# A plain column order in the first matmul behind the scan, and two scaled blocks moved behind the last sums

## The chip, the cores and the metric

The kernel runs on one core of one Trainium2 chip. The metric is the device time of one execution in microseconds. The kernel before takes 1699.45 us, the median of three runs (1698.41 to 1699.90).

## What is computed

The trunk has one layer here (`DEPTH = 1`), so the reference comes down to an attention branch between two norms:

```python
x1   = rms_norm(x, norm_attn)                      # 256 rows, 4096 columns, float32
proj = x1 @ w_in                                   # 4096 x 16384 -> q | k | v | gate
o    = stick_breaking_attention(q, k, v)           # 32 heads of 128, strictly causal
h    = x + (o * silu(gate)) @ w_out                # 4096 x 4096
out  = rms_norm(h, final_norm)
```

In a head, `z = q k' / sqrt(128)`, the weight of position s for row t is `sigmoid(z[t,s])` times the product of `1 - sigmoid(z[t,j])` over s < j < t, and the kernel forms that product as a sum of logarithms: the "scan" over positions, which TensorE does with a triangle of ones as one operand.

## The kernel before

**Tiling.** The rows are two blocks, t = 0 (rows 0-127) and t = 1 (rows 128-255). The columns of `w_in` are worked in 16 units of two heads (q, k, gate and v columns of both), those of `w_out` in 4 units. A unit runs over 16 steps of 256 of the 4096 summed elements. In a step the 2 x 2 x 2 block products are done as eight plain products or, in most steps, as seven by sums and differences of blocks. Each product adds a 128x512 result into one PSUM bank (`acc`).

**One product is three matmuls.** Every float32 operand is split into a rounded high part and the rest (`wh`, `wl` for the weights; `sh`, `sl` or `oh`, `ol` for the rows). `mm3` (line 813) issues high x high, high x low, low x high, each 128x512. The profile writes them `acc<-wh,sh`, `acc<-wl,sh`, `acc<-wh,sl`.

**The order of columns.** A matmul may take its 512 columns in any order, if it reads and writes them in the same one. A word of three letters gives the order of a product's three matmuls. "e" takes groups of eight neighbouring columns: the first group of each 32 columns, then the second of each 32, in four rounds. "c" does the same with groups of four and of each 16 columns. Which word a product gets is set in `product` (line 1234): it counts the products since other matmuls ran (`since_others`). The first seven behind such matmuls get the words of `BEHIND_OTHERS` (line 37). Later the first product of a step gets "cce" or "ecc", and all others "eee".

**The other matmuls.** `ten` (line 345) issues the groups of the attention between products and sets the count to zero. A head has four groups: `turn` (transposes of q and k), `scores` (z), `scan` (line 879: four matmuls with the triangle and a transpose of the gate), and `out_of_head` (line 909: the sum over v, and a transpose). There are 32 heads, so 32 scans, all while `w_in`'s products and the first of `w_out`'s run.

**Order of the work.** A planner written in the kernel (`Plan`) simulates the engines with its own costs when the program is built, and emits each engine's instructions in the order in which they would start. Each piece of work has a due time as its key; a piece that is not ready is passed over, and on the chip each engine then runs its own queue strictly in that order.

**The end.** The last five parts are finished bank by bank (`LAST_ORDER`), so that rows 128-255 are complete first: their sums, squares, mean, root (`part_done`, `finish`) and scaling (`rows_out`, line 1201) run while TensorE still works on rows 0-127. The last bank (3, rows 0-127) is added in two halves of 256 columns. `joined` (line 1173) then makes the mean but for the last 256 columns and tells `("most", t)`; `finish` waits for that, takes the root on ScalarE, one Newton step on VectorE, and starts `rows_out` for the eight blocks of 512 columns of that t. Blocks 6 and 7 still lack the gain and are scaled by one VectorE instruction with two factors; the others by VectorE or ScalarE. Each block then goes out by a DMA that SyncE issues.

Of the kernel before, what the change touches and what calls it, by code (L numbers as in the profile page):

```python
# [19 lines left out]
P = 128  # L20
# [13 lines left out]

ROUNDS = 4
RUNS = {"e": 8, "c": 4}
BEHIND_OTHERS = ("ccc", "ecc", "eee", "eee", "eee", "eee", "cce")
IN_STEP = ("cce", "ecc")
WARM, IDLE = 10, 640
# [69 lines left out]
def tensor_ns(n):  # L109
    return 0.4167 * n + 8.5 if n > 128 else 109.0  # L110
# [138 lines left out]
def kernel(  # L249
# [10 lines left out]
    nc = Plan(tc)  # L260
# [50 lines left out]
    for g, (n, k) in enumerate(order):  # L311
        p = parts[n]
# [17 lines left out]
    def dve(emit, n, key=None, more=0, **kw):  # L330
        n = n if isinstance(n, tuple) else (n,)
        cost = sum(vector_ns(m) for m in n) + 122 * (len(n) - 1) + more
        return nc.work("vector", cost, emit, soon() if key is None else key, **kw)

    def act(emit, n, key=None, **kw):
        n = n if isinstance(n, tuple) else (n,)
        cost = sum(scalar_ns(m) for m in n) + 100 * (len(n) - 1)
        return nc.work("scalar", cost, emit, soon() if key is None else key, **kw)
# [1 line left out]

    FULL_P, FULL_S = (P,) * 2, (W,) * 2

    since_others = 0

    def ten(emit, *n):
        def others():
            nonlocal since_others
            since_others = 0
            emit()

        return nc.work("tensor", 40 + sum(tensor_ns(m) for m in n), others, nc.here - 1e4, wait=400)

    def moved(engine, emit, sizes, key, after=None, hold=False, adds=False, wait=0):
        issue = 550 if engine == "gpsimd" else 330
        return nc.work(
            engine, issue * len(sizes), emit, key, after=after, hold=hold, moves=[(4 * P * n, adds) for n in sizes],
            wait=wait,
        )
# [454 lines left out]
    def mm3(out_, a, b, start, stop, orders):  # L813

        (ah, al), (bh, bl) = a, b
        for k, (x, y) in enumerate(((ah, bh), (ah, bl), (al, bh))):
            to, y = (t.rearrange("p (h q e) -> p q h e", q=ROUNDS, e=RUNS[orders[k]]) for t in (out_, y))
            nc.tensor.matmul(to, x, y, start=start and k == 0, stop=stop and k == 2, skip_group_check=True)


    BW = 3 * P
    not_before = off.broadcast_to([P, 2, P])

    def head(u, i):
# [3 lines left out]
        def turn():  # L828
            for k in range(2):
                for t in range(NT):  # L830
                    c = k * CW + i * P
                    nc.tensor.transpose(tr[:, k, t * P : (t + 1) * P], st["qk", u][:, t, c : c + P], ident)

        yield ten(turn, P, P, P, P)
        if i == HG - 1:
            nc.give("one")
# [10 lines left out]
        def scores():  # L847
# [4 lines left out]
            nc.tensor.matmul(diagonal, ident_b, not_before, start=False, **kw)  # L852

        yield ten(scores, *FULL_P, *FULL_S, 2 * P)
        nc.give("gh")
        yield nc.take("gh", sooner=True)
# [22 lines left out]
        def scan():  # L879
# [4 lines left out]
            nc.tensor.matmul(z[:, 2 * P : BW], neg_one, fl[:, 0:P], stop=True, **kw)  # L884
            turned(gT, 0)

        yield ten(scan, BW, BW, P, P, P)
        nc.give("gh", "gh")
        if i == 0:
            yield nc.take("gh", sooner=True)  # L890
# [34 lines left out]
    def heads(u):  # L925
        nc.start(gate(u))
        yield nc.until(("qk", u))
        for i in range(HG):
            yield from head(u, i)

        nc.tell(("heads", u))
        if u < NS - 1:
            spill[u] = dp.tile([P, 4, P], F32, name=f"spill{u}")
            yield moved(
                "gpsimd", lambda: nc.gpsimd.dma_start(spill[u], st["o", u]), [4 * P], soon(),
                after=lambda: (nc.give("gh"), nc.tell(("spilled", u))),
            )
# [46 lines left out]
    hs, xres, grow = {}, {}, {}  # L984
# [186 lines left out]
    most = {}  # L1171
# [8 lines left out]
    def finish(last, t, late):  # L1180
        v, r, f = (scalar_of_rows() for _ in range(3))
        second = ssq_h[:, t, NJ : NJ + 1]

        def root():
            nc.scalar.activation(r, second, AF.Ln, scale=1.0 / D, bias=most[t])
            nc.scalar.activation(r, r, AF.Exp, scale=-0.5)

        yield act(root, (1, 1), late - 2)

        def factor():  # L1190
            nc.vector.scalar_tensor_tensor(
                out=v, in0=second, scalar=1.0 / D, in1=most[t], op0=ALU.mult, op1=ALU.add
            )
            e = newton(r, v, f"rout{t}")
            nc.vector.tensor_tensor(out=f, in0=r, in1=e, op=ALU.mult)

        yield dve(factor, (1, 1, 1, 1), late - 2)
        for k, c in enumerate(range(NJ)):
            nc.start(rows_out(c, t, f, late + 100 * (NT - t) + k))

    def rows_out(c, t, f, key):
        h = hs[c, t]
        if c >= NJ - 2:
            yield nc.until(("grow", c))
            yield dve(
                lambda: nc.vector.scalar_tensor_tensor(
                    out=h, in0=h, scalar=f, in1=grow[c], op0=ALU.mult, op1=ALU.mult
                ),
                W, key,
            )  # L1210
        elif c in ON_SCALAR[t]:
            yield act(lambda: nc.scalar.activation(h, h, AF.Copy, scale=f), W, key)
        else:
            yield dve(
                lambda: nc.vector.tensor_scalar(out=h, in0=h, scalar1=f, scalar2=None, op0=ALU.mult), W // 2, key
            )
        yield moved("sync", lambda: nc.sync.dma_start(out[t * P : (t + 1) * P, c * W : (c + 1) * W], h), [W], key)
# [16 lines left out]
    def product(n, k):  # L1234
        nonlocal since_others
        p = parts[n]
        b, f, c = p["prods"][k]
        h, l = forms[p["s"]]
        orders = "eee"
        if since_others < len(BEHIND_OTHERS):  # L1240
            orders = BEHIND_OTHERS[since_others]
        elif p["i"] == 0 and k == 0:
            orders = IN_STEP[p["s"] % len(IN_STEP)]
        since_others += 1
        mm3(
            ev[p["u"]][b],
            (h[:, PLACES[f], :], l[:, PLACES[f], :]),
            tuple(t[:, c].rearrange("p i n -> p (i n)") for t in (wh[n], wl[n])),
            starts[p["u"], b] == (n, k),
            ends[p["u"], b] == (n, k),  # L1250
            orders,
        )

    def products():
        for g, (n, k) in enumerate(order):
            p = parts[n]
            u, s = p["u"], p["s"]
            b, f, c = p["prods"][k]
            if u < 1:
                what = "s"  # L1260
            elif u < OUT0:
                what = "n"
            elif u == OUT0:
                what = "o"
            else:
                what = "r" if u == LAST and s in EIGHT_LAST else "p"
            if starts[u, b] == (n, k):
                yield nc.take(f"b{b}")
                ev.setdefault(u, {})[b] = acc.tile([P, W], F32, tag=f"b{b}", name=f"acc{u}_{b}")
            yield nc.until(("low", n, c), ("form", what, s), lead=nc.LEAD)  # L1270
            yield nc.work(
                "tensor", PRODUCT, lambda: product(n, k), g * PRODUCT, after=lambda n=n, k=k: done(n, k), hold=False
            )
            nc.here = g * PRODUCT
# [59 lines left out]
```

## Time and profile before

| | |
|---|---|
| runs, median (lowest to highest) | 1699.45 us (1698.41 to 1699.90) |
| the profiled execution | 1698.9 us |
| its span, first to last instruction | 1697.1 us |
| TensorE busy | 1680.2 us, 99%, 7776 matmuls |
| VectorE busy | 1602.0 us, 94% |
| ScalarE busy | 1206.7 us, 71% |
| granted TensorE clock, mean | 0.997 |
| DMA | 412.77 MB, 243 GB/s |

PE is TensorE's matmuls, PEld its weight loads, DVE VectorE, ACT ScalarE, POOL GpSimd, SP SyncE. The timeline gives for each instruction its start and its time in microseconds from the start of the span. A matmul's end is modelled and runs into the next one, so the rate of TensorE is read from the distance between two starts, not from the busy share. The profile shows shapes, not the order of columns: that is read from the kernel's code, by counting products behind a group of other matmuls. The kernel issues nearly everything through one helper, so all rows name line 132 and are told apart by their tiles: `z` is the bank of scores and scan, `o` the bank of a head's result, `acc` the products, `h` the rows of the result, `sq` the squares, `scalars` the means, roots and factors.

### The profile page before, as it was taken

To read this page: it belongs to the slowest core of one execution; us is meant where nothing else is said; L and a number is where in the kernel's file an instruction comes from. 1 tells how busy PE (TensorE), PEld (TensorE's weight loads), DVE (VectorE), ACT (ScalarE), POOL (GpSimd) and SP (SyncE) were. 2 spreads that over 40 slices of the span, in tenths; PEclk is the share of its full clock that TensorE was granted. 3 is DMA by queue.
4 is the path that set the end of the run, shared out by engine and by line. 5 is a ranking of instruction groups with operands and counts; after the bars stand their busy time and mean duration, and the time that the engine had idled before them with its cause. 6 is when DMAs were issued, how large, how long until landed. Compare 5 with 4: busy or idle time off the path is not lost.

```text
span 1697.1 us, 25128 instructions
## 1 busy us (share of the span) xinstructions
PE 1680.2 (99%) x7776; PEld 1417.4 (84%) x7776; DVE 1602.0 (94%) x2025; ACT 1206.7 (71%) x1665; POOL 324.9 (19%) x400
## 2 busy tenths in 40 slices
PE   9999999999999999999999999999999999999997
PEld 7888888888888888888888888888888888888885
DVE  8899999999999999999999999999999978999997
ACT  8986767676767676767676767676868775656654
POOL 0012222121222222222212121212122111212110
PEclk9999999999999999999999999999999999999998
DMA  9978888878787878797978797979797978888895
GB/s 343 332 197 247 232 247 222 252 217 253 215 256 212 256 212 266 199 272 196 276 201 269 198 268 196 272 198 269 204 264 210 300 230 266 245 245 256 246 304 185
DMA packets 248438, 412.77 MB, mean 243 GB/s; under 512 B 28016, under 2 KB 72560, under 8 KB 248304
## 3 DMA queue, kind: packets, MB, share of 16 engines
q1 hardware_dynamic: 194544, 354.24, 62.7%
q0 software_dynamic: 53472, 56.65, 20.0%
q8 instruction: 61, 1.00, 0.2%
q14 instruction: 73, 0.60, 0.1%
q10 hardware_dynamic: 288, 0.28, 0.1%
HBM read 402.93 MB, written 8.13 MB: 242 GB/s over the span
## 4 chain that ended last, share of the span: by engine, by line
PE 94%; DVE 3%; DMA 1%; issue 1%; ACT 1%; SPq 0%; DVEq 0%; ACTq 0%
PE acc L132 89%; PE z L132 3%; PE o L132 1%; DVE wl L132 1%; PE tr L132 1%; DVE h L132 1%; DVE raw L132 0%; ACT wh L132 0%; DMA raw<-in_w_out_dram 0%; DMA raw<-in_w_in_dram 0%; DMA xres<-in_x_dram 0%; SPq L132 0%; ACT sq L132 0%; DVE scalars L132 0%; DVE qk_sb L132 0%
## 5 line engine op out<-in xcount | busy, mean ns | idle before, releaser
L132 ACT CAST wh<-raw 128x1024 fp32r<-128x1024 f32 (+1 forms) x989 | 919.3, 970 | 385.5 <-DVE raw L132 160.9
L132 DVE TENSOR_TENSOR wl<-raw,wh 128x1024 fp32r<-128x1024 f32 (+1 forms) x815 | 975.7, 1220 | 49.3 <-ACT wh L132 23.9
L132 PE MATMUL acc<-wh,sh 128*128 128x512 f32 x2048 | 771.9, 389 | 0.1
L132 PE MATMUL acc<-wh,sl 128*128 128x512 f32 x1898 | 727.1, 383 | 1.8 <-DVE sl L132 1.8
L132 PE MATMUL acc<-wl,sh 128*128 128x512 f32 x1748 | 668.9, 383 | 0.1
L132 PEld LDWEIGHTS acc<-wh,sh 128*128 128x128 f32 x2048 | 384.0, 188 | 77.9 <-DVE qk_sb L132 4.9
L132 POOL DMA_DIRECT2D raw<-in_w_in_dram x300 | 258.3, 947 | 972.2 <-DMA raw<-in_w_in_dram 375.1
L132 PEld LDWEIGHTS acc<-wh,sl 128*128 128x128 f32 x1898 | 356.0, 188 | 66.3 <-DVE sl L132 2.4
L132 PEld LDWEIGHTS acc<-wl,sh 128*128 128x128 f32 x1748 | 328.4, 188 | 55.6 <-DVE wl L132 0.4
L132 DVE TENSOR_TENSOR raw<-raw,raw 128x512 f32<-128x512 f32 x348 | 238.3, 688 | 15.3 <-DMA raw<-in_w_in_dram 11.7
L132 PE MATMUL acc<-wh,oh 128*128 128x512 f32 x512 | 192.4, 383 | 0.0
L132 PE MATMUL acc<-wh,ol 128*128 128x512 f32 x488 | 186.7, 383 | 0.0
L132 PE MATMUL acc<-wl,oh 128*128 128x512 f32 x464 | 177.6, 383 | 1.4 <-DVE wl L132 1.4
L132 DVE TENSOR_TENSOR wh<-raw,wh 128x512 fp32r<-128x512 f32 x174 | 119.7, 688 | 3.3 <-ACT wh L132 2.7
L132 DVE TENSOR_TENSOR raw<-raw 128x512 f32<-128x512 f32 x174 | 119.4, 686 | 0.0
L132 PEld LDWEIGHTS acc<-wh,oh 128*128 128x128 f32 x512 | 96.1, 188 | 17.3
L132 PEld LDWEIGHTS acc<-wh,ol 128*128 128x128 f32 x488 | 91.5, 188 | 16.1
L132 PEld LDWEIGHTS acc<-wl,oh 128*128 128x128 f32 x464 | 87.1, 188 | 17.6 <-DVE wl L132 2.2
L132 POOL DMA_DIRECT2D raw<-in_w_out_dram x48 | 41.5, 984 | 173.8 <-DMA raw<-in_w_out_dram 85.2
L132 ACT ACTIVATE f<-f 128x384 f32<-128x384 f32 x96 | 50.5, 526 | 3.0
L132 POOL DMA_DIRECT2D p<-spill x27 | 17.0, 676 | 89.9 <-DVE ol L132 32.0
L132 DVE SCALAR_TENSOR_TENSOR gv_sb<-acc,scalars,gv_sb 128x512 f32<-128x512 f32 x45 | 33.5, 745 | 0.0
(86 smaller groups left out, 765.7 us busy)
## 6 DMA issues: line engine op xcount, KB each, us to landing
raw<-in_w_in_dram SPq DMA_DIRECT2D x1024, 256.0 KB, 4.5
raw<-in_w_out_dram SPq DMA_DIRECT2D x256, 256.0 KB, 4.5
raw<-in_w_in_dram POOLq DMA_DIRECT2D x300, 128.0 KB, 5.2
p<-spill POOLq DMA_DIRECT2D x27, 256.0 KB, 4.6
raw<-in_w_out_dram POOLq DMA_DIRECT2D x48, 128.0 KB, 5.4
xr<-in_x_dram SPq DMA_DIRECT2D x16, 256.0 KB, 5.3
xres<-in_x_dram SPq DMA_DIRECT2D x16, 256.0 KB, 5.5
out_dram<-h SPq DMA_DIRECT2D x16, 256.0 KB, 2.8
```

What stands on the lines that cost most here:

```text
L132: return self.tc.keep_in_program_order(getattr(self.engine, name)(*args, **kw))
```

## The change

Behind a scan, and only there, the words of the first two products change from "ccc", "ecc" to "rcc", "eee". The letter "r" is not in `RUNS`: `mm3` then leaves the 512 columns in their plain order. The words from the third product on stay as they were. In `rows_out`, blocks 6 and 7 wait for `("most", 0)` beside their gain. For rows 0-127 that has been told by then; for rows 128-255 it places the two instructions behind rows 0-127's last sums and `joined` on VectorE.

```diff
+BEHIND_SCAN = ("rcc", "eee")
 BEHIND_OTHERS = ("ccc", "ecc", "eee", "eee", "eee", "eee", "cce")
...
-    since_others = 0
-
-    def ten(emit, *n):
+    since_others, words = 0, BEHIND_OTHERS
+
+    def ten(emit, *n, behind=BEHIND_OTHERS):
         def others():
-            nonlocal since_others
-            since_others = 0
+            nonlocal since_others, words
+            since_others, words = 0, behind + BEHIND_OTHERS[len(behind) :]
             emit()
...
         for k, (x, y) in enumerate(((ah, bh), (ah, bl), (al, bh))):
-            to, y = (t.rearrange("p (h q e) -> p q h e", q=ROUNDS, e=RUNS[orders[k]]) for t in (out_, y))
+            if orders[k] in RUNS:
+                to, y = (t.rearrange("p (h q e) -> p q h e", q=ROUNDS, e=RUNS[orders[k]]) for t in (out_, y))
+            else:
+                to = out_
...
-        yield ten(scan, BW, BW, P, P, P)
+        yield ten(scan, BW, BW, P, P, P, behind=BEHIND_SCAN)
...
         if c >= NJ - 2:
-            yield nc.until(("grow", c))
+            yield nc.until(("grow", c), ("most", 0))
...
-        if since_others < len(BEHIND_OTHERS):
-            orders = BEHIND_OTHERS[since_others]
+        if since_others < len(words):
+            orders = words[since_others]
```

## The prediction

> **What bounds the kernel.** I read the page first (engines, chain that ended last), then the windows by stage, then TensorE's timeline.
>
> ```profile
> PE 1680.2 (99%) x7776; PEld 1417.4 (84%) x7776; DVE 1602.0 (94%) x2025; ACT 1206.7 (71%) x1665; POOL 324.9 (19%) x400
> ...
> PE 94%; DVE 3%; DMA 1%; issue 1%; ACT 1%; SPq 0%; DVEq 0%; ACTq 0%
> ...
> 50.00:1400.00 1350.00, 1349.91 (x6298) 1141.17 (x6298) 1288.64 (x1580) 988.22 (x1346) 275.30 (x331) 1.00 0.83 238
> ```
>
> Between 50 and 1400 us TensorE never stands still and has its full clock (1.00). All 32 scans lie there, so a nanosecond saved between two matmul starts is a nanosecond of the kernel: nothing hides it, and no other engine has to become faster. The question is how far apart the starts are. In an undisturbed stretch (timeline, first row and the thirteenth after it):
>
> ```profile
> 1000.06 0.38 PE L132 MATMUL acc<-wl,sh 128*128 128x512 f32 x1
> ...
> 1002.92 0.38 PE L132 MATMUL acc<-wh,sl 128*128 128x512 f32 x1
> ```
>
> 2.86 us over 13 is 0.220 us a matmul, in groups of eight. Behind a scan it is different:
>
> ```profile
> 297.26 0.34 PE L132 MATMUL z<-fh,neg_tri 128*128 128x384 f32 x1
> 297.44 0.34 PE L132 MATMUL z<-fl,neg_tri 128*128 128x384 f32 x1
> ...
> 297.84 0.47 PE L132 MATMUL acc<-wh,sh 128*128 128x512 f32 x1
> 298.15 0.39 PE L132 MATMUL acc<-wl,sh 128*128 128x512 f32 x1
> ...
> 298.60 0.39 PE L132 MATMUL acc<-wh,sh 128*128 128x512 f32 x1
> 298.82 0.38 PE L132 MATMUL acc<-wl,sh 128*128 128x512 f32 x1
> ...
> 299.27 0.39 PE L132 MATMUL acc<-wh,sh 128*128 128x512 f32 x1
> 299.51 0.39 PE L132 MATMUL acc<-wl,sh 128*128 128x512 f32 x1
> ...
> 299.97 0.38 PE L132 MATMUL acc<-wh,sh 128*128 128x512 f32 x1
> ```
>
> The product matmuls are numbered 0 to 8 here, the ninth interval ending at 299.97. Together 2.13 us, where nine at 0.220 would be 1.98: 0.15 too long. Of that, 0.09 is interval 0 (0.31); the other 0.06 is spread over 1 to 8, most of it in the three "eee" of the third product (299.27 to 299.97: 0.70 for 0.66). These are the same columns in the same groups of eight as at 1000 us, but slower: the stream has a rhythm that the scan upsets and that comes back at matmul 9. The last scan shows the same total, 2.13:
>
> ```profile
> 1398.92 0.47 PE L132 MATMUL acc<-wh,oh 128*128 128x512 f32 x1
> ...
> 1401.05 0.38 PE L132 MATMUL acc<-wh,oh 128*128 128x512 f32 x1
> ...
> L132 PE MATMUL z<-ident,gv_sb 128*128 128x128 f32 x32 | 9.5, 297 | 0.0
> ```
>
> Of the 32, 31 have it within 0.01; only the first takes another course:
>
> ```profile
> 105.09 0.47 PE L132 MATMUL acc<-wh,sh 128*128 128x512 f32 x1
> 105.40 0.38 PE L132 MATMUL acc<-wl,sh 128*128 128x512 f32 x1
> ...
> 106.07 0.38 PE L132 MATMUL acc<-wl,sh 128*128 128x512 f32 x1
> ...
> 106.52 0.60 PE L132 MATMUL acc<-wh,sh 128*128 128x512 f32 x2
> ...
> 107.19 0.38 PE L132 MATMUL acc<-wh,sh 128*128 128x512 f32 x1
> ```
>
> 2.10 us with the same words. From 105.40, "c c e" costs 0.67, and the "eee" from 106.52 also 0.67, within 0.01 of the undisturbed 0.66: here the rhythm is back at once. So two courses exist; the order of columns and the few nanoseconds in which the group ends choose between them.
>
> **The change, part by part.** *Word 0, "ccc" to "rcc"* (32 matmuls). The trace has no plain row of 512 at this rate; the nearest is the scan's own plain row of 384 (297.26 to 297.44: 0.18). By columns that is 0.24 for 512, by adding 128 columns at 0.220/512 it is 0.23. Interval 0 is 0.31 whatever its order, since it holds the weight loads that the four short matmuls ahead left no time for. I take zero, for 0.23 is below 0.31; the ends are +0.02 us a scan (0.24 less an undisturbed 0.22) and -0.09 (all of interval 0's excess).
>
> The Trainium skill has a rule that speaks for the plain row: "PSUM — Partial Sum Buffer", Specifications, says that any access that is not contiguous slows matmuls significantly. By it each plain row would be faster than one in groups. The trace doesn't agree: 0.18/384 is 0.47 ns a column plain, 0.220/512 is 0.43 in groups of eight. By the rule 32 plain rows would bring at most those -0.09 us a scan, 2.9 us.
>
> *Word 1, "ecc" to "eee"* (64 matmuls from groups of four to eight). Matmuls 1 to 3 stay "c c e": 0.67 in the one course (298.15 to 298.82), 0.67 in the other. From 4 on all are "e". In the good rhythm intervals 4 to 8 are 5 x 0.220 = 1.10. Sum from the start of matmul 0: 0.31 + 0.67 + 1.10 = 2.08 against 2.13, -0.05 a scan. The other end on this side is that the slow three come anyway (0.70 for 0.66): 2.12, -0.01. On the far side the slow spacing (0.70/3 = 0.233) goes on; that is a rival below. I take -0.05, because what is dropped is a second change of grouping, and both courses above pay 0.01 or more for each "c c e". 32 x -0.05 = -1.6 us, unrounded starts giving about -1.5.
>
> *What follows the scan.* `out_of_head` comes 12 or more matmuls later and upsets the stream anew. It too has two courses, 2.10 and 2.12 over its first nine:
>
> ```profile
> 109.84 0.47 PE L132 MATMUL acc<-wh,sh 128*128 128x512 f32 x1
> ...
> 111.94 0.38 PE L132 MATMUL acc<-wh,sh 128*128 128x512 f32 x1
> ...
> 125.84 0.47 PE L132 MATMUL acc<-wh,sh 128*128 128x512 f32 x1
> ...
> 127.96 0.38 PE L132 MATMUL acc<-wh,sh 128*128 128x512 f32 x1
> ```
>
> If the scan's new course flips half of the 32, that is 16 x 0.02, +/-0.3 us; I take 0.
>
> *The two scaled blocks.* No instruction is added; two of VectorE's move, and two DMA issues with them.
>
> ```profile
> 1684.93 0.42 DVE L132 TENSOR_TENSOR h<-acc,h 128x256 f32<-128x256 f32 x1
> 1685.26 0.74 DVE L132 SCALAR_TENSOR_TENSOR h<-h,scalars,grow 128x512 f32<-128x512 f32 x1
> 1685.92 0.42 DVE L132 TENSOR_TENSOR h<-acc,h 128x256 f32<-128x256 f32 x1
> 1686.25 0.15 DVE L132 SCALAR_TENSOR_TENSOR scalars<-squares_of_rows,scalars 128x1 f32<-128x1 f32 x1
> 1686.97 0.16 DVE L132 SCALAR_TENSOR_TENSOR scalars<-squares_of_rows,scalars 128x1 f32<-128x1 f32 x1 [0.57 <-ACT sq L132]
> 1687.54 0.22 DVE L132 SCALAR_TENSOR_TENSOR scalars<-scalars 128x1 f32<-128x1 f32 x1 [0.40 <-ACT scalars L132]
> 1687.79 0.15 DVE L132 TENSOR_SCALAR scalars<-scalars 128x1 f32<-128x1 f32 x1
> ...
> 1685.44 0.39 ACT L132 ACTIVATE sq<-h 128x256 f32<-128x256 f32 x1 [1.68 <-DVE h L132]
> 1685.76 0.19 ACT L132 ACTIVATION_READ_ACCUMULATOR sq<-h 128x1 f32 x1
> 1686.43 0.39 ACT L132 ACTIVATE sq<-h 128x256 f32<-128x256 f32 x1 [0.48 <-DVE scalars L132]
> ```
>
> Today a block (0.66 to the next start) stands between the two halves of the last sum. Without it the second half starts at 1685.26 instead of 1685.92. Its squares then wait only for ScalarE, free at 1685.95: 0.45 earlier than 1686.43, and the root with them. But the blocks come next: `joined` (today 1686.25, 0.15 long) at 1685.98, the blocks some 0.2 later at 1686.17 and 1686.83, the first step of `factor` (now 1686.97, in an idle stretch) at 1687.49, and the Newton step 0.25 later (as 1687.54 to 1687.79, the step after it), 1687.74, against 1687.54. The 0.45 of the root is swallowed, and the step that used to lie in a gap now follows two blocks: **+0.2 us**. The planner keeps this order, since by its own costs the blocks (600 ns each) are ready before the second squares and the root are through.
>
> ```profile
> 1688.69 4.45 SPq L132 DMA_DIRECT2D out_dram<-h x8
> ...
> 1684.00:1688.50 4.50, 1.00 1.03 382
> ...
> 1689.25:1689.50 0.25, 0.50 0.16 49
> 1689.50:1694.00 4.50, 0.50 1.02 380
> ```
>
> SyncE's eight issues for rows 0-127 (from 1688.69) move by those 0.2. The DMA engines are full up to 1689.25 with rows 128-255, run empty for a moment and are full again: the end follows rows 0-127's first issue. The two moved issues, at about 1687.0 and 1687.6, still arrive while that first stream runs. Ends: -0.45 (if `factor` came ahead of the blocks) and +0.4 (if the two blocks also reach the DMA engines too late for the first stream).
>
> **The sum** goes against the profiled execution (1698.9 us: the span of 1697.1 and 1.8 around it): -1.5 + 0.2 = -1.3, so 1697.6. The median of the runs is 0.55 higher; against it, 1698.1.
>
> **Rivals.** *A, the rhythm stays upset (slower).* If "eee" from matmul 4 falls into the slow spacing and only the next attention matmuls end it, intervals 4 to 11 (or to 14, for the second head of a unit) cost 0.233 each. Against today's five intervals (1.15, 298.82 to 299.97) and then 0.220 that is 8 x 0.233 - 1.15 - 3 x 0.22 = 0.05, or 0.09 with eleven: 0.07 x 32 = +2.2 us. With the plain row's 0.02 (0.6 us) and the end's 0.2 that is +3.0: 1702.5. It is slower than before as soon as more than five of the intervals are slow. For it: three slow "e" in a row stand in the trace behind the scan. Against: they end by themselves at the third.
>
> *B, the words don't matter.* The slow intervals belong to the scan's short matmuls, not to the order. Then only the end is left, with up to -0.3 from the words: 1699.4. For it: 31 of 32 scans run alike. Against: the scan at 105 us, and equal shapes at 0.22 and 0.233. The Trainium skill has this rival as a rule: "TensorE: Matmul & The Clock Gate", "Wait — 56ns, not 53.3ns?", gives 215.7 ns from start to start for 512 columns at full clock and knows no order of columns. By this rule words are worth nothing; this trace, with 220 to 233 ns at a clock of 1.00, doesn't agree.
>
> *C, the gain spreads.* The words "cce" and "ecc" stand at the head of some 220 of the 320 steps as well, and "c c e" cost 0.01 over 0.66 above. If the new course met them in a state in which that is saved, it would be 220 x 0.01 = -2.2 us on top: 1695.9. Against: the other attention groups reset the stream in between.
>
> **Chances.** Forecast 0.55, A 0.15, B 0.22, C 0.08. About 0.2% (3.4 us) is what a measurement of this kernel can tell from no change; only the far halves of A and C go beyond it, so slower 0.07, faster 0.06, same 0.87. The forecast's own range is 1697.2 to 1699.0 (its ends by the scan's -1.7 to -1.1, the end's 0.4 and 0.5 of spread between runs). The range over the cases leaves out the far halves of A and C: 1696.2 to 1701.8.
>
> **What would show it.** Right: behind the scans the start of matmul 9 comes 2.08 us after matmul 0, with no interval over 0.225 from 4 on; between the two halves of the last sum nothing stands, and the Newton step comes 2.8 us after the first half (now 2.61). Wrong: intervals of 0.23 beyond matmul 8 (A), 2.13 as before (B), another spacing at places that the change does not touch (C), an interval 0 above 0.32 (the plain row is not hidden).

## The result, and the profile after

The changed kernel takes 1701.97 us (median of 16 runs, 1701.02 to 1704.36), the kernel before 1698.78 us (16 runs, 1697.31 to 1700.80). The ratio is 1.0019 with a 95% interval of [1.0011, 1.0027]: 3.2 us slower. The prediction said 1698.1. Its sign was wrong, and the measured time lies just above its range. Its rival A, sized at 1702.5, is what happened.

The page of the changed kernel, engines and chain:

```profile
PE 1685.0 (99%) x7776; PEld 1417.7 (83%) x7776; DVE 1603.8 (94%) x2025; ACT 1207.2 (71%) x1665; POOL 324.7 (19%) x400
...
PE 95%; DVE 2%; DMA 1%; issue 1%; ACT 0%; SPq 0%; DVEq 0%; ACTq 0%
```

Its window of 50 to 1400 us (columns: stretch, length, busy time and count of PE, PEld, DVE, ACT, POOL, granted clock, DMA share, GB/s):

```profile
50.00:1400.00 1350.00, 1350.00 (x6283) 1138.03 (x6282) 1289.20 (x1579) 987.57 (x1345) 273.91 (x328) 1.00 0.83 237
```

TensorE is still never idle there and its clock is still 1.00, but it gets through 6283 matmuls where it got through 6298. Fifteen matmuls at 0.22 us are 3.3 us: the whole loss is matmuls that start further apart, at full clock. The timeline of the changed kernel (start, time, instruction) shows them behind the scan that the prediction quoted:

```profile
298.25 0.48 PE L133 MATMUL acc<-wh,sh 128*128 128x512 f32 x1
298.57 0.39 PE L133 MATMUL acc<-wl,sh 128*128 128x512 f32 x1
...
299.25 0.39 PE L133 MATMUL acc<-wl,sh 128*128 128x512 f32 x1
...
300.40 0.40 PE L133 MATMUL acc<-wh,sh 128*128 128x512 f32 x1
300.63 0.39 PE L133 MATMUL acc<-wl,sh 128*128 128x512 f32 x1
...
301.55 0.40 PE L133 MATMUL acc<-wh,sl 128*128 128x512 f32 x1
301.79 0.82 PE L133 MATMUL o<-a,gv_sb 128*128 128x256 f32 x4
...
302.47 0.48 PE L133 MATMUL acc<-wh,sh 128*128 128x512 f32 x1
...
304.60 0.38 PE L133 MATMUL acc<-wh,sh 128*128 128x512 f32 x1
```

Matmul 9 starts at 300.40, 2.15 us after matmul 0, where 2.08 was predicted and 2.13 stood before. And the stream does not recover there. From matmul 4 (299.25) to the next attention group (301.79) eleven intervals take 2.54 us: 0.231 each, in groups of eight that ran at 0.220 elsewhere. The next group of short matmuls ends it. (Behind the last two scans, where 36 and more matmuls follow, the words at matmul 18 are "cce" again: the last stream came back some matmuls later, the other one did not.) The unrounded starts give this course for the first intervals behind a scan, in ns:

| kernel | intervals 0 to 8 | 9, 10, 11 |
|---|---|---|
| before (31 of 32 scans) | 309 226 220 228 223 226 233 232 232 | 221 219 221 |
| after (31 of 32 scans) | 314 228 223 232 229 236 222 230 230 | 237 228 229 |
| after, scan at 105 us | 319 219 230 225 219 221 219 221 219 | 221 219 221 |

Added up over all 32 scans, from matmul 0 to the next attention group: 111.06 us before, 113.39 after, **+2.33 us**, of which 0.48 stands behind the last two scans. The first nine intervals behind `out_of_head` (302.47 to 304.60 above: 2.13) went from 2105 to 2129 ns in the mean, **+0.77 us** over 32. Scores (-0.3), transposes (+0.3) and the end (+0.05) are small. That is the 3.2 us. The profiled execution itself took 1704.36 us, the longest of the 16. It holds 1.8 us more of waits in `w_out`'s stage (at 1518, 1569 and 1585 us) than the profile of before; the other 15 runs took 1702.74 us at most.

The end, VectorE in the changed kernel's timeline:

```profile
1690.28 0.76 DVE L133 TENSOR_TENSOR h<-acc,h 128x256 f32<-128x256 f32 x2 [0.53 <-PE acc L133]
1691.34 0.16 DVE L133 SCALAR_TENSOR_TENSOR scalars<-squares_of_rows,scalars 128x1 f32<-128x1 f32 x1 [0.30 <-ACT sq L133]
1691.42 1.41 DVE L133 SCALAR_TENSOR_TENSOR h<-h,scalars,grow 128x512 f32<-128x512 f32 x2
1692.74 0.15 DVE L133 SCALAR_TENSOR_TENSOR scalars<-squares_of_rows,scalars 128x1 f32<-128x1 f32 x1
1693.00 0.22 DVE L133 SCALAR_TENSOR_TENSOR scalars<-scalars 128x1 f32<-128x1 f32 x1
```

Both halves of the last sum now run on end, `joined` (1691.34) and the two blocks (1691.42) follow, and the first step of `factor` (1692.74) comes behind them. The Newton step (1693.00) comes 2.72 us after the first half, where it came 2.61 before and 2.8 was predicted.

### The profile page after: what moved, and what is told of

The parts are those of the page before. It is cut to its first block, busy times and chain, and to the rows that moved or that the text cites. A ratio compares the mean times of both kernels' runs of the same rounds, so it can differ in the third digit from the quotient of the medians.

```text
span 1702.6 us, 25128 instructions
## 1 busy us (share of the span) xinstructions
PE 1685.0 (99%) x7776; PEld 1417.7 (83%) x7776; DVE 1603.8 (94%) x2025; ACT 1207.2 (71%) x1665; POOL 324.7 (19%) x400
## 4 chain that ended last, share of the span: by engine, by line
PE 95%; DVE 2%; DMA 1%; issue 1%; ACT 0%; SPq 0%; DVEq 0%; ACTq 0%
PE acc L133 90%; PE z L133 3%; PE o L133 1%; DVE wl L133 1%; PE tr L133 1%; DMA raw<-in_w_out_dram 1%; DVE h L133 1%; DVE raw L133 1%; DMA raw<-in_w_in_dram 0%; DMA xres<-in_x_dram 0%; ACT wh L133 0%; SPq L133 0%; DVE wh L133 0%; DVE scalars L133 0%; ACT sq L133 0%
```

## The experiments

Two theories for the scan's part stood against each other: the plain row upsets the stream (P), or the earlier groups of eight do, since groups of four are what brings it back (E). A third possibility was that none of it is the order of columns, but what the other engines and the DMAs do at that moment. "Quick" below is the spacing of 0.220 us in groups of eight, "slow" that of 0.230 to 0.231. The edits are shown against the changed kernel; of the runs with TensorE alone some of the new lines are shown. In all whole kernels but e_tail the blocks of the end are where they were before. A unit has two heads, called first and second here.

**The plain row alone (e_plain).**

```diff
-BEHIND_SCAN = ("rcc", "eee")
+BEHIND_SCAN = ("rcc", "ecc")
```

> Words behind the scan 'rcc', 'ecc' (the plain row alone; the two blocks stay where they were). Theory P (the plain row upsets the rhythm): the intervals behind the scan start 0.314, 0.228, 0.223, 0.232 us as in the changed kernel and stay at 0.23 beyond matmul 8; the first nine sum to 2.14 us or more, time +2 to +3 us over before. Theory E (the second product in eights no longer brings the rhythm back; the plain row itself is harmless): intervals 9 to 11 are 0.22 each as before, the first nine 2.13 to 2.15 us, time within 0.5 us of before.

1700.63 against 1698.95 us, ratio 1.0011 [1.0002, 1.0021]. Its timeline, matmuls 0, 9 and 12:

```profile
297.76 0.48 PE L133 MATMUL acc<-wh,sh 128*128 128x512 f32 x1
...
299.91 0.39 PE L133 MATMUL acc<-wh,sh 128*128 128x512 f32 x1
...
300.60 0.39 PE L133 MATMUL acc<-wh,sh 128*128 128x512 f32 x1
```

Nine intervals 2.15, the next three 0.69: slow, though the groups of four at matmuls 4 and 5 are all there. The stretch to the next group is 2.14 us longer over all scans, of the change's 2.33. So one letter does most of the scans' part, as P has it. It does not do the whole 3.2: the time is 1.7 us above before, under the 2 to 3 that P expected, and the first nine intervals behind `out_of_head` are 2106 ns in the mean, as before. The +0.77 there does not come from the plain row alone.

**The groups of eight alone (e_eights).**

```diff
-BEHIND_SCAN = ("rcc", "eee")
+BEHIND_SCAN = ("ccc", "eee")
```

> Words behind the scan 'ccc', 'eee' (no plain row, the second product in eights; the two blocks stay). Theory P: the first four intervals are before's 0.309, 0.226, 0.220, 0.228 and the rhythm is back at once or after three eights: the first nine sum to 2.08 to 2.12 us, intervals 9 to 11 are 0.22, time 0.3 to 1.5 us under before. Theory E: intervals 4 to 11 are 0.23, the first twelve sum to 0.05 to 0.08 us more than before's 2.79, time +2 to +3 us.

1699.76 against 1698.95 us, 1.0009 [1.0000, 1.0018]. Its timeline, matmuls 0, 9, 10 and 12:

```profile
298.34 0.47 PE L133 MATMUL acc<-wh,sh 128*128 128x512 f32 x1
...
300.48 0.39 PE L133 MATMUL acc<-wh,sh 128*128 128x512 f32 x1
300.71 0.38 PE L133 MATMUL acc<-wl,sh 128*128 128x512 f32 x1
...
301.15 0.38 PE L133 MATMUL acc<-wh,sh 128*128 128x512 f32 x1
```

One more slow interval (300.48 to 300.71: 0.23), then 0.44 for two: it comes back without a group of four. Over all scans +0.61 us. So E is not the main cause; but the gain that the prediction hoped for from these words is not there either, and `out_of_head` stays at 2105 ns. The two parts do not simply add: behind the scans 2.14 and 0.61 alone, 2.33 together; behind `out_of_head` nothing alone, 0.77 together.

**The blocks alone (e_tail).**

```diff
-BEHIND_SCAN = ("rcc", "eee")
+BEHIND_SCAN = ("ccc", "ecc")
```

(here the moved blocks stay moved)

> Words as before, only the two blocks moved behind the last sums. Both theories: intervals behind the scans as before; the Newton step 3.15 us after the start of the last matmul (before 3.10), the end 0.05 us later, time within 0.1 us of before but for the spread between runs. If the two blocks were a part of the 3.2 us, it would be 0.5 us or more slower.

1698.31 against 1698.95 us, 0.9998 [0.9989, 1.0008]: no difference that this measurement can tell. From the last matmul's start to the Newton step it is 3.15 us, in the changed kernel 3.15 too, before 3.10: the moved blocks cost 0.05 us.

**TensorE alone (m_rhythm).** The same kinds of matmul, with operands loaded once and nothing else running; 21 pairs of words (`firsts`) behind each of the four groups, each case behind a scan with the same words (`RESET`), and a few longer runs.

```diff
+    for g in ("scan", "scores", "turn", "out"):
+        for f in firsts:
+            out.append(("scan", RESET))
+            out.append((g, f + eee * 8))
...
+    out.append(("scan", ("rcc", "eee", "eee", "cce") + eee * 12))
...
+    out.append(("scan", ("rcc",) + eee * 30))
```

> TensorE's matmuls alone: real weights and rows in SBUF, streams of products with weight loads as in the kernel, and between them the four groups of short matmuls, each followed by 21 pairs of words; the rest of the layer is left out, and the output holds one PSUM bank. If the rhythm is TensorE's own, the words of before give 0.309, 0.226, 0.220, 0.228, 0.223, 0.226, 0.233, 0.232, 0.232, 0.221 us behind the scan and those of after 0.314, 0.228, 0.223, 0.232, 0.229, 0.236 and so on, as in the kernels. If it comes from the other engines' or the DMAs' use of SBUF, all streams run alike at 0.216 to 0.220 us. Long streams without any group: eights 0.220 (as in the kernel), fours between 0.218 and 0.230, plain 0.230 to 0.24 by the scan's row of 384. By theory P a plain first row is slow with every second word, by theory E every first word is slow that is followed by eights alone.

The intervals of the two kernels come out again, to within a nanosecond or two: 309 226 220 228 223 225 234 231 233 221 219 behind a scan with "ccc ecc", and 315 227 223 232 229 236 223 230 230 236 228 229 with "rcc eee". Windows of this kernel, two of the stream behind "rcc eee" (matmuls 0 to 9, and 24 intervals from matmul 5) and the same two of the stream behind "cee eee":

```profile
81.70:83.85 2.15, 2.15 (x12) 1.78 (x12) 0.00 (x0) 0.00 (x0) 0.00 (x0) 1.00 0.00 0
82.93:88.46 5.53, 5.53 (x26) 4.52 (x24) 0.00 (x0) 0.00 (x0) 0.00 (x0) 1.00 0.00 0
244.90:246.98 2.08, 2.08 (x12) 1.78 (x12) 0.00 (x0) 0.00 (x0) 0.00 (x0) 1.00 0.00 0
246.10:251.38 5.28, 5.28 (x26) 4.50 (x25) 0.00 (x0) 0.00 (x0) 0.00 (x0) 1.00 0.00 0
```

5.53 over 24 is 0.2304, 5.28 over 24 is 0.2200, with VectorE, ScalarE and GpSimd at zero, no DMA and the clock at 1.00. So neither other engines nor transfers are needed for it. Both spacings keep themselves up: behind "rcc" and eights alone the slow one lasted as long as the run did, 93 matmuls. With "rcc eee eee cce" instead, the stream was back at 0.220 right behind the last word. And "cee eee", one row in groups of four and then eights, was quick from matmul 2 on. The next runs put such words into the kernel.

**Fours at matmuls 6 and 7 (e_end_fours).**

```diff
-BEHIND_SCAN = ("rcc", "eee")
+BEHIND_SCAN = ("rcc", "eee", "cce")
```

> Words behind the scan 'rcc', 'eee', 'cce' (the changed kernel's, with groups of four put into the third product; the two blocks stay). Theory S (two steady rhythms of the eights, 0.220 and 0.2305; a stream keeps the one that it is in until two fours in a row come at a matmul that takes it out): intervals 0 to 5 as in the changed kernel (0.314 to 0.236), then 0.234, 0.239, 0.225 or near it, and 0.220 from matmul 9 on; 0.5 to 1.5 us over before instead of 3.2. Theory L (the plain row loses the stream for a fixed time): intervals 9 to 11 stay at 0.23 whatever the third product is; 3 us over before.

1702.17 against 1698.85 us, 1.0020 [1.0011, 1.0029]. Its timeline, matmuls 0, 6, 9 and 12:

```profile
298.21 0.48 PE L133 MATMUL acc<-wh,sh 128*128 128x512 f32 x1
...
299.67 0.39 PE L133 MATMUL acc<-wh,sh 128*128 128x512 f32 x1
...
300.35 0.39 PE L133 MATMUL acc<-wh,sh 128*128 128x512 f32 x1
...
301.04 0.39 PE L133 MATMUL acc<-wh,sh 128*128 128x512 f32 x1
```

The recovery that was hoped for did not come. "cce" takes 0.68 (299.67 to 300.35), the three eights behind it still 0.69. Groups of four do not by themselves end the slow spacing; it matters when they come.

**One row in groups of four, then eights (e_one_four).**

```diff
-BEHIND_SCAN = ("rcc", "eee")
+BEHIND_SCAN = ("cee", "eee")
```

> Words behind the scan 'cee', 'eee' (one matmul in fours, all others in eights; the two blocks stay). Theory S, with the intervals of the streams run alone: 0.309, 0.228, then 0.219 and 0.221 in turn, nine of them 2.076 us against before's 2.129: -0.053 x 32 = -1.7 us, and what the next group makes of it, -0.5 to +0.5 us. Theory L2 (in the whole kernel eights alone behind a group always fall into the slow rhythm, as in the changed kernel and with 'ccc', 'eee'): 0.23 from matmul 2 on, 2 to 3 us slower than before.

1697.35 against 1698.85 us, 0.9990 [0.9981, 0.9999]. Its timeline, matmuls 0, 1 and 9:

```profile
297.23 0.47 PE L133 MATMUL acc<-wh,sh 128*128 128x512 f32 x1
297.54 0.39 PE L133 MATMUL acc<-wl,sh 128*128 128x512 f32 x1
...
299.30 0.38 PE L133 MATMUL acc<-wh,sh 128*128 128x512 f32 x1
```

2.07 us for nine intervals, in all 32 scans, and quick from there: -1.68 us over all scans, -1.5 measured. The 2.08 that the prediction wanted from "rcc eee" can be had, with another first word.

**Such words behind three groups (e_all_groups).**

```diff
-BEHIND_SCAN = ("rcc", "eee")
+BEHIND_SCAN = BEHIND_OUT = ("cee", "eee")
+BEHIND_SCORES = ("eee", "eee")
...
-        yield ten(scores, *FULL_P, *FULL_S, 2 * P)
+        yield ten(scores, *FULL_P, *FULL_S, 2 * P, behind=BEHIND_SCORES)
...
-        yield ten(out_of_head, *FULL_P, *FULL_S, P)
+        yield ten(out_of_head, *FULL_P, *FULL_S, P, behind=BEHIND_OUT)
```

> The scan and the out-of-head group followed by 'cee', 'eee', the scores by 'eee', 'eee', the transposes as before; the two blocks stay. Theory S: nine intervals 2.076 us behind the scan (before 2.129), 2.066 behind the scores (before 2.114 to 2.136), 2.069 behind the out-of-head group (before 2.092 to 2.114): -0.053, -0.060 and -0.035 us, together -0.148 x 32 = -4.7 us: 1694. Theory L2: the eights behind these groups stay slow, 5 us or more slower.

1705.17 against 1698.85 us, 1.0037 [1.0025, 1.0050]: the slowest of all, where 1694 was hoped for. The words had been quick with TensorE alone. Here "eee eee" was quick behind the scores of second heads (308 219 219 221) and slow behind those of first heads (311 228 233 226 ... 230), with one exception each. "cee eee" was slow behind 28 of the 32 `out_of_head` (first nine 2143 ns in the mean of all), and also behind 15 scans, 12 of them of second heads, where e_one_four had it quick. Same words, same short matmuls ahead. The unrounded starts show a difference of 1 to 2 ns in the time from the scan's first short matmul to matmul 0: among first heads 569 ns in the quick ones and 571 in the slow ones, among second heads 577 to 578 in the quick ones and 579 in the slow ones (the first heads of the first and the last unit stand apart: 581 and 578, quick).

**The same words three products later (e_fours_later).**

```diff
-BEHIND_SCAN = ("rcc", "eee")
+BEHIND_SCAN = ("rcc", "eee", "eee", "cce")
```

> Words behind the scan 'rcc', 'eee', 'eee', 'cce': the two fours one product later than in the last try, at matmuls 9 and 10, where TensorE's streams alone came back to 0.220 (0.234, 0.239, 0.225, 0.221). Theory S2 (the slow rhythm is a state that a stream keeps; fours take it out only if they meet it at the right point of its cycle of five or six intervals): intervals 0 to 8 as in the changed kernel, 9 to 11 at 0.234, 0.239, 0.225, and for every second scan, which has 15 products' matmuls behind it, 0.220 from 12 on instead of 0.230; time 1.5 to 2.7 us over before. Theory L (lost for a fixed time whatever comes): 12 to 14 stay at 0.230, 3.2 us over before.

1698.86 against 1698.52 us, 1.0000 [0.9991, 1.0010], less than the 1.5 to 2.7 us over that were expected. The letters of the first nine matmuls are those of the changed kernel, but its timeline has two courses. A first head, matmuls 0 and 9, and a second head, matmuls 0, 1 and 9:

```profile
278.44 0.48 PE L133 MATMUL acc<-wh,sh 128*128 128x512 f32 x1
...
280.58 0.39 PE L133 MATMUL acc<-wh,sh 128*128 128x512 f32 x1
...
297.86 0.48 PE L133 MATMUL acc<-wh,sh 128*128 128x512 f32 x1
298.18 0.38 PE L133 MATMUL acc<-wl,sh 128*128 128x512 f32 x1
...
299.95 0.38 PE L133 MATMUL acc<-wh,sh 128*128 128x512 f32 x1
```

2.14 and 2.09. The scans of 14 second heads take the quick one, 314 220 230 225 219 221, where the changed kernel had the slow one in all of them; the first scan, at 105 us, was quick in both. With identical letters at the same scan, what differs by the trace is how the scan's group ends: by the unrounded starts it takes 579 to 580 ns from its first short matmul to matmul 0 in these 14, and 577 to 578 in the two second heads that are slow, as in the changed kernel. Across heads that time tells nothing: first heads have 569 to 570 (the last 578) and are slow. That the few nanoseconds choose the course, and do not only go with it, is not shown. In first heads the "cce" at 9 ends the slow spacing, and the `out_of_head` behind takes the quicker course (2.096) in all but the first and the last unit.

**Orders and operands, TensorE alone (m_orders).** Each order once behind a quick stream (`RESET`) and once behind a slow one (`SLOW`).

```diff
+RESET = ("cee", "eee", "eee", "eee", "eee")
+SLOW = ("rcc", "eee", "eee", "eee", "eee")
...
+for o in ["e", "c", "r"] + [k for k in ORDERS if k not in "ec"] + list(SIDES) + ["x", "y", "z", "X", "Y", "Z", "1", "2"]:
+    for lead in (RESET, SLOW):
+        out.append(("scan", lead))
+        out.append(("-", (3 * o,) * 12))
```

> TensorE's matmuls alone again (all else left out, the output holds one PSUM bank): 23 orders of columns and the plain one in streams of 36, each once behind a stream in the quick rhythm and once behind one in the slow rhythm; then streams in which only the reads or only the writes are in groups, streams with the stationary operand 16, 32 and 64 bytes further, and streams in one bank. Theory S: eights run at 0.220 or 0.2305 us by what stood before. If the rhythm is a meeting of the moving operand's reads with the weight loads in SBUF, ordered reads alone keep the two rhythms and ordered writes alone run like the plain row (0.2267), and a shift of the stationary operand changes the spacing. If it is PSUM's, it is the other way round, and one bank or four makes a difference. Some other order may run at 0.216 to 0.218.

Windows of 24 intervals each: eights behind quick, eights behind slow, plain rows; only the reads in groups of eight behind quick and behind slow, only the writes; then eights with the stationary operand 16, 32 and 64 bytes further on:

```profile
34.59:39.87 5.28, 5.28 (x25) 4.50 (x24) 0.00 (x0) 0.00 (x0) 0.00 (x0) 1.00 0.00 0
46.74:52.28 5.54, 5.54 (x26) 4.53 (x24) 0.00 (x0) 0.00 (x0) 0.00 (x0) 1.00 0.00 0
83.34:88.78 5.44, 5.44 (x26) 4.51 (x24) 0.00 (x0) 0.00 (x0) 0.00 (x0) 1.00 0.01 3
683.94:689.22 5.28, 5.28 (x26) 4.50 (x24) 0.00 (x0) 0.00 (x0) 0.00 (x0) 1.00 0.00 0
696.08:701.62 5.54, 5.54 (x26) 4.53 (x24) 0.00 (x0) 0.00 (x0) 0.00 (x0) 1.00 0.00 0
708.34:713.78 5.44, 5.44 (x25) 4.51 (x24) 0.00 (x0) 0.00 (x0) 0.00 (x0) 1.00 0.00 0
781.80:787.49 5.69, 5.69 (x26) 4.53 (x25) 0.00 (x0) 0.00 (x0) 0.00 (x0) 1.00 0.00 0
806.75:812.19 5.44, 5.44 (x25) 4.53 (x24) 0.00 (x0) 0.00 (x0) 0.00 (x0) 1.00 0.00 0
831.25:836.75 5.50, 5.50 (x26) 4.52 (x25) 0.00 (x0) 0.00 (x0) 0.00 (x0) 1.00 0.00 0
```

Divided by 24: 0.220 and 0.231 for the eights by what stood before them, 0.227 for plain rows from either side. Reads in groups of eight alone give the same two values. Writes alone run as plain rows do. So the two spacings belong to how the moving operand is read, and not to the order of the writes into PSUM. The bank written is not without effect: with all matmuls into one bank, eights took 0.231 behind either stream, so the quick spacing was not kept there; plain rows took 0.227 as before. The last three rows differ in nothing but where the stationary operand lies: 0.237, 0.227 and 0.229, each the same behind either stream. (They cycle through three stationary blocks where the first rows use four, so they are compared with one another.) Plain rows took 0.233 at all three places. None of 21 other groupings was faster than quick eights.

**Which words find the quick spacing (m_chain).** Fifteen first words by two second words, TensorE alone, behind `out_of_head` 12 and 15 matmuls after a scan, and behind scores 9 and 18 matmuls after the transposes.

```diff
+for w in words:
+    for second in ("eee", "ecc"):
+        rest = (w, second) + 5 * eee
+        out += [("scan", RESET + ("ecc",)), ("scan", ("cee",) + 3 * eee), ("out", rest)]
+        out += [("scan", RESET), ("scan", ("cee",) + 4 * eee), ("out", rest)]
+        ...
```

> TensorE's matmuls alone (all else left out, the output holds one PSUM bank): the out-of-head group 12 and 15 matmuls behind a scan with 'cee', 'eee', and the scores 9 and 18 matmuls behind the transposes, each with 15 first words and two second ones. Theory S2 says that no word is good everywhere: the same word gives 0.220 or 0.23 by the distance from the last group, since that decides with which few nanoseconds the group ends. If the word alone decided, each would give the same nine intervals at both distances.

The same word is quick or slow by the distance. Behind `out_of_head`, "eee eee" takes 2159 ns for nine intervals at 12 matmuls and 2068 at 15, "cee ecc" 2069 at 12 and 2135 at 15. Only "ece" was quick in all four places: with "eee" behind it 2093 and 2095, and 2077 and 2073 behind the scores. (Behind a scan, in m_rhythm, the same "ece eee" was slow, 2160.)

**The words that held (e_scan_scores, e_scan_scores_out).** These were chosen not for the widest gain at one place, but because their course did not depend on the distance: "ece" in m_chain, "cee" behind all scans of e_one_four.

```diff
-BEHIND_SCAN = ("rcc", "eee")
+BEHIND_SCAN = ("cee", "eee")
+BEHIND_SCORES = ("ece", "eee")
...
-        yield ten(scores, *FULL_P, *FULL_S, 2 * P)
+        yield ten(scores, *FULL_P, *FULL_S, 2 * P, behind=BEHIND_SCORES)
```

and in e_scan_scores_out also

```diff
-        yield ten(out_of_head, *FULL_P, *FULL_S, P)
+        yield ten(out_of_head, *FULL_P, *FULL_S, P, behind=BEHIND_SCORES)
```

> Scan followed by 'cee', 'eee' and scores by 'ece', 'eee'; the rest as before, the two blocks stay. In the streams of TensorE alone 'ece' kept the quick rhythm at both distances tried: 2.075 us over nine behind the scores, where before has 2.114 to 2.136. Theory S2, if the scores' group ends in the whole kernel as in those streams: -0.053 and -0.05 us for each of 32 heads, -3.3 us: 1695.3, nine intervals at 2.07 to 2.08 behind both. Against it (the first heads' scores come after waits and end otherwise): those 16 stay slow and the gain is -1 to -2 us, or it is gone.

> As e_scan_scores, and 'ece', 'eee' behind the out-of-head group too, where the streams alone gave 2.093 to 2.095 at both distances (before 2.092 and 2.114). Theory S2: another -0.3 us, 1695.0, and no nine intervals over 2.10 behind it. Against it: with eights alone to follow, some of these groups fall into the slow rhythm up to the next group, +0.1 us each, and the gain is smaller than without.

e_scan_scores takes 1696.07 against 1698.98 us, 0.9983 [0.9974, 0.9993]. With "ece eee" behind `out_of_head` as well it is 1695.75, 0.9981 [0.9972, 0.9990]: 3.2 us faster than before where the change was 3.2 slower. The step from e_scan_scores to this is too small to be told apart. The timeline of e_scan_scores_out, matmuls 0 and 9 behind the scores and behind the scan:

```profile
182.21 0.47 PE L134 MATMUL acc<-wh,sh 128*128 128x512 f32 x1
...
184.29 0.38 PE L134 MATMUL acc<-wh,sh 128*128 128x512 f32 x1
...
297.21 0.47 PE L134 MATMUL acc<-wh,sh 128*128 128x512 f32 x1
...
299.29 0.38 PE L134 MATMUL acc<-wh,sh 128*128 128x512 f32 x1
```

2.08 in both. 31 of the 32 scans and 30 of the 32 scores take a quick course here; the other three show that even these words are not safe everywhere. In the mean over the kernel the first nine intervals go from 2132 to 2080 ns behind the scores, from 2128 to 2078 behind the scans and from 2105 to 2094 behind `out_of_head`: (52 + 50 + 11) x 32 is 3.6 us. To the next group it is 3.3, since the two slow streams behind scores go on losing, and 3.2 are measured.

## Why the prediction was wrong

**The bound held.** "A nanosecond saved between two matmul starts is a nanosecond of the kernel": the intervals from each attention group to the next, added up, gave the measured difference: +3.2 for +3.2 in the changed kernel, +1.9 for +1.7 with the plain row alone, -1.5 for -1.5 in e_one_four, -3.3 for -3.2 in e_scan_scores_out; the worst is -2.3 for -2.9 in e_scan_scores.

**The step that failed** is the term 1.10 in the sum 0.31 + 0.67 + 1.10: five quick intervals from matmul 4 on. In the changed kernel the three terms measured 0.314, 0.683 and 1.147, so the stream was in the slow spacing there, and it stayed in it: +0.015 us in the first nine intervals and another 0.03 for each three beyond them. 32 scans cost +2.33 us where -1.5 was predicted. Two choices led to that term, and each was undone alone.

- *Zero for Word 0.* As a price in its own interval it held: the plain row costs 5 ns there (314 for 309), with 0.02 us as the bound. (A stream of plain rows has 0.227 us in m_orders, a little under the 0.23 to 0.24 that were estimated.) But the sum took zero for the whole word. With the plain row alone (e_plain) the stretch up to the next group gets 2.14 us longer, 0.067 a scan. The first row goes on to set the spacing of the matmuls behind it, and the prediction had no term for that.
- *-0.05 for Word 1*, "because what is dropped is a second change of grouping". That assumed that without a second change the stream would be quick from matmul 4, whatever stood before. Alone (e_eights) it cost +0.61 us where it was to bring the -1.5.

The trace of before had offered the scan at 105 us as the model of a stream that is back at once. That scan is the one of 32 that took the quick course in the changed kernel too. It was a sign that the same words can go either way, and was read as a sign of what the new words would do.

**Rival A had the mechanism, and the argument against it was a misreading.** "They end by themselves at the third": the three intervals of 0.233 in the kernel before are the end of a course that leads into the quick spacing. The slow spacing is another state, which does not end by itself within 93 matmuls. A priced the scan's part at 2.2 and 0.6 us, measured +2.33 together, 0.48 of it behind the last two scans, whose longer stretches A did not count; its end at 0.2, measured 0.05. What A did not have is `out_of_head`: "I take 0 (+/-0.3)" measured +0.77, since nearly all of the 32 took courses that the trace of before does not have behind this group, 2.13 us over nine intervals where 2.10 and 2.11 had been seen. The total of 3.0 came out near 3.2 by luck: the errors offset.

**Rival B fell.** The scan's stretch moved between -1.68 and +2.33 us, and the kernel between 1695.75 and 1705.17, by words alone. The Trainium skill's rule that stood beside B ("TensorE: Matmul & The Clock Gate", "Wait — 56ns, not 53.3ns?") gives one spacing for 512 columns at full clock; with TensorE alone at a clock of 1.00 these runs have 0.220, 0.227 and 0.231 us by order and history, so it does not agree. **Rival C** fell as well: behind `out_of_head` the first nine intervals cost 0.77 us, and the whole stretches up to the next group, 739 us in all, 0.81. That leaves nothing for the heads of the steps in them.

**The end held in mechanism, its size did not.** The second half's squares and the root are earlier, the blocks come ahead of `factor`, and the gain is swallowed, as written. +0.2 was predicted, +0.05 measured: the first half began 0.43 us after the last matmul's start, not 0.49, and the blocks 0.08 after `joined`'s start, not 0.2.

**The range** took A's far half out, which is where the time fell. With two steady courses in view, and the choice between them unexplained, 0.15 for A was too little: nothing in the profile of before said which of them a new word would take.

## What to carry to other kernels

When an engine is never idle and at full clock, read the distance between starts behind each disturbance, and up to the next one: a stream can settle in a slower spacing that costs little per instruction (10 ns here) and need not end by itself (here not in 93 matmuls). If two courses of the same instructions stand in one trace, treat a new order as a coin to be thrown on the chip, not as a sum of prices; and prefer an order that is quick in all the places and distances tried to one that is quickest in one. Undoing a change in parts also showed that one letter makes most of the scans' loss (2.14 of 2.33 us) and about half of the kernel's (1.7 of 3.2), and that a neighbour of it gains.

## What the runs showed of the hardware

- Matmuls of 512 float32 columns, read in groups of eight, have two steady spacings at full clock, 0.220 and about 0.231 us. Plain rows had 0.227 from either. Which of the two a stream takes depends on the order of its first few matmuls, and goes with the last few nanoseconds of what stood before it: letters that were slow behind 14 scans of the changed kernel were quick behind the same scans in e_fours_later, with the scan's group 1 to 3 ns longer.
- The two spacings come with the reads of the moving operand in groups of eight (reads alone: 0.220 and 0.231; writes alone: 0.227). For such reads the spacing depends on where the stationary operand lies: 0.237, 0.227 and 0.229 at 16, 32 and 64 bytes further on, where plain rows have 0.233 at all three. With one PSUM bank for all matmuls only 0.231 was seen. The Trainium skill ("TensorE: Matmul & The Clock Gate", "Step-by-step: what each phase is for") says that loading the next weights does not take read bandwidth from the running matmul. If that were all there is to it, the place of the weights should not show in the spacing; in these three rows it does.
- Of PSUM, the memory that a matmul writes, the Trainium skill says that any access that is not contiguous slows matmuls significantly ("PSUM — Partial Sum Buffer", Specifications). Here, groups of eight in the writes alone ran at 0.227, as plain rows did. Groups of two, in reads and writes both, took 0.43 to 0.46; which of the two sides makes that, no run here shows.
- What happens inside, why the groups of short matmuls end some nanoseconds apart, and so which words are quick in another kernel, is open. No run here shows it.
